# A two-layer hybrid decoder trunk: where weights are split, which banks the gates use, and when gated outputs are turned

## The chip, the cores and the metric

The kernel runs on one core of a Trainium2 chip. The metric is the device time of one execution in microseconds (us); three runs of the kernel before gave 1159.62 to 1160.34 us, with a median of 1159.97 us. Five engines share the work: TensorE (PE in the profile; PEld is its weight load), VectorE (DVE), ScalarE (ACT), GpSimd (POOL) and SyncE (SP), which here issues the transfers from device memory (DMA). Sums of products land in PSUM, in eight banks of 128 x 512 fp32 numbers.

## The reference

256 tokens of 1024 numbers pass through two layers. Each layer has a mixer and a mixture of experts:

```python
proj = h @ w_in[l]
(c_q, c_kv, k_rope, dn_qkv, dn_beta, dn_a, dn_gate,
 hg_q, hg_f, hg_i, hg_gate, gate_logits) = jnp.split(proj, SPLIT_POINTS, axis=-1)
y_a = mla_branch(c_q, c_kv, k_rope, ...) @ w_br_a[l]       # latent attention, 8 heads
y_b = gated_deltanet_branch(dn_qkv, ..., dn_gate, ...) @ w_br_b[l]
y_c = hgrn2_branch(hg_q, hg_f, hg_i, hg_gate, ...) @ w_br_c[l]
g_a, g_b, g_c = jnp.split(jax.nn.sigmoid(gate_logits), N_BRANCHES, axis=-1)
mixed = (g_a * y_a + g_b * y_b + g_c * y_c) @ w_out[l]
h = layer_norm(DEEPNORM_ALPHA * h + mixed, ln1_g[l], ln1_b[l])
moe_out = hier_moe(h, ...)         # top 1 of 4 groups, then top 2 of its 8 experts of width 256
h = layer_norm(DEEPNORM_ALPHA * h + moe_out, ln2_g[l], ln2_b[l])
```

The outputs of the deltanet and HGRN2 branches are normalised per head and multiplied by silu of their gates (dn_gate, hg_gate) before w_br_b and w_br_c.

## The kernel before

**Splitting.** The mixer's products keep fp32 precision by writing each operand as a high part (fp32r) and a remainder. For a weight piece of 128 x 1024, `split` (L241) makes the high part wh with a copy on ACT (L249) and the remainder wl with a subtraction (L250). The subtraction is on DVE, except for four pieces of a layer named in `POOLED` (L143), where POOL does it: both pieces of chunk cq (the first projection), one of the first merge gate, one of the deltanet gate. `mm3` then issues three products: high by high, high by low, low by high (L261 to L263). wh and wl have two buffers each.

**Layer.** A layer (L589) starts with the hidden state in token rows. Two diagonal matrices hold each token's 1/deviation (L619); multiplied by them on PE, the state is turned and scaled at once (L395), evacuated by ACT and DVE (L401, L403), and split into hTh and hTl (L254, L255). Then come the chunks of the input projection and the three branches in the order of the list `seq`, `merge_branch` a, the gates of both remaining branches, `branch_gate` (normalise, gate, turn the gated outputs by L1126), merges b and c, and `project_out` with the router's products. Weights arrive in tiles of 128 x 2048 fp32 (1 MB), four buffers at a time; when the mixer's pool `mp` closes, `open_prefetch` takes its memory for 13 tiles more, first the rest of the mixer's weights and then the first experts'.

**Banks.** A wide product (256 tokens x 512 columns) accumulates in two banks. `ps("pa")` hands out pa and po in turn; pb and pm have three banks each, which go to scans, turns and small sums. Every gate, merge and output product thus takes the pair pa, po, and the next one may start in a bank when DVE or ACT has read the last.

**Clock products.** `warm(n)` issues n bf16 products of 128 x 512 whose result nobody reads (L365). They stand after the turned state in layer 0 (8 of them) and at the end of layer 0's experts (14).

**Experts.** They run in quads, with 1 MB tiles of gate, up and down weights streaming in through rotating buffers (L1602, L1635). A scheduler orders each engine's instructions by the program's order and dependencies; `issue_after` keeps an instruction behind a given one.

## Time and profile before

| what | value |
|---|---|
| median of 3 runs | 1159.97 us |
| the profiled execution | 1160.61 us |
| its span | 1158.8 us |
| PE, DVE, ACT, POOL busy | 91%, 50%, 37%, 14% |
| mixer of layer 0, about | 0 to 376 us |
| experts of layer 0, about | 376 to 577 us |
| mixer of layer 1, about | 578 to 945 us |
| experts of layer 1, about | 945 to 1137 us |

An execution is 1.8 us longer than its span. A busy share is a mean over stages; so the stages are read apart. In a timeline, a bracket at a row's end tells how long the engine had been idle and what ended that. The matmuls' ends are modelled: in an unbroken row of 512-column products one lasts 0.40 us and the next starts 0.23 to 0.24 us after it, so an idle time in a bracket is 0.16 us shorter than what the start of the row was late.

### The profile page before, as it was taken

To read this page: it belongs to the slowest core of one execution; us is meant where nothing else is said; L and a number is where in the kernel's file an instruction comes from. 1 tells how busy PE (TensorE), PEld (TensorE's weight loads), DVE (VectorE), ACT (ScalarE), POOL (GpSimd) and SP (SyncE) were. 2 spreads that over 40 slices of the span, in tenths; PEclk is the share of its full clock that TensorE was granted. 3 is DMA by queue.
4 is the path that set the end of the run, shared out by engine and by line. 5 is a ranking of instruction groups with operands and counts; after the bars stand their busy time and mean duration, and the time that the engine had idled before them with its cause. 6 is when DMAs were issued, how large, how long until landed. Compare 5 with 4: busy or idle time off the path is not lost. (4 is left out here: it accounts for less than half of the span.)

```text
span 1158.8 us, 21407 instructions
## 1 busy us (share of the span) xinstructions
PE 1059.3 (91%) x8896; PEld 775.6 (67%) x8896; DVE 576.9 (50%) x1269; ACT 427.3 (37%) x788; POOL 162.7 (14%) x146
## 2 busy tenths in 40 slices
PE   7999999999999998777889999999999999977775
PEld 5888987777777664434378889777777766543442
DVE  7677754575556422111276876645754562321114
ACT  5764632554445211111067545235444351211111
POOL 2111025101210400000020110450021112000001
PEclk9999999999999999898899999999999999989997
DMA  7632250549965999999983214315599679999994
GB/s 231 200 107 73 91 165 2 169 158 359 424 271 220 410 425 426 426 426 427 366 230 106 74 46 138 110 38 182 196 411 374 251 270 425 426 425 426 427 426 190
DMA packets 104706, 305.58 MB, mean 264 GB/s; under 512 B 20962, under 2 KB 48028, under 8 KB 79516
## 3 DMA queue, kind: packets, MB, share of 16 engines
q1 hardware_dynamic: 104604, 304.15, 68.4%
q8 instruction: 72, 1.18, 0.4%
q14 instruction: 30, 0.25, 0.1%
HBM read 303.08 MB, written 1.05 MB: 262 GB/s over the span
## 5 line engine op out<-in xcount | busy, mean ns | idle before, releaser
L250 DVE TENSOR_TENSOR wl<-w,wh 128x1024 fp32r<-128x1024 f32 x150 | 187.0, 1248 | 161.5 <-ACT wh L249 161.0
L249 ACT CAST wh<-w 128x1024 fp32r<-128x1024 f32 x158 | 165.7, 1049 | 217.7 <-PE ps_po L263 74.7
L1602 PE MATMUL ps_pa<-w,xg 128*32 128x256 f32 x2304 | 175.1, 436 | 59.0 <-DMA w<-in_exp_w_up_dram 29.4
L1602 PEld LDWEIGHTS ps_pa<-w,xg 128*32 128x32 f32 x2304 | 88.0, 125 | 140.4 <-DMA w<-in_exp_w_up_dram 38.2
L1614 DVE SCALAR_TENSOR_TENSOR hm<-ps_pa,ws,hm 128x256 f32<-128x256 f32 x18 | 8.7, 484 | 203.5 <-ACT hm L1613 203.3
L1613 ACT ACTIVATE hm<-ps_pa 128x256 f32<-128x256 f32 x18 | 6.9, 384 | 221.8 <-PE ps_pa L1602 221.8
L261 PE MATMUL ps_pa<-wh,hTh 128*128 128x512 f32 x176 | 71.2, 405 | 2.0 <-ACT hTh L254 0.7
L261 PE MATMUL ps_po<-wh,hTh 128*128 128x512 f32 x176 | 71.2, 405 | 1.9 <-ACT hTh L254 0.7
L262 PE MATMUL ps_po<-wl,hTh 128*128 128x512 f32 x176 | 70.5, 401 | 2.1 <-DVE wl L250 1.6
L262 PE MATMUL ps_pa<-wl,hTh 128*128 128x512 f32 x176 | 70.5, 401 | 2.1 <-DVE wl L250 1.6
L1635 PE MATMUL ps_pm<-w,hmT 128*32 128x512 f32 x576 | 70.8, 595 | 1.3 <-issue 1.3
L263 PE MATMUL ps_pa<-wh,hTl 128*128 128x512 f32 x176 | 70.0, 398 | 0.2 <-DVE hTl L255 0.2
L263 PE MATMUL ps_po<-wh,hTl 128*128 128x512 f32 x176 | 69.9, 397 | 0.2 <-DVE hTl L255 0.2
L1552 PEld LDWEIGHTS ps_pm<-P,h1c 128*128 128x128 f32 x576 | 66.8, 192 | 2.2 <-ACT res L1350 1.0
L1552 PE MATMUL ps_pm<-P,h1c 128*128 128x128 f32 x576 | 67.3, 275 | 0.0
L1561 ACT ACTIVATE xg<-ps_pm,gb 128x128 f32<-128x128 f32 x72 | 32.9, 458 | 71.7 <-DVE xg L1559 71.7
L1574 POOL TENSOR_TENSOR Pw<-P,small 128x128 f32<-128x128 f32 x32 | 12.4, 405 | 306.9 <-PE ps_pm L1581 227.9
L1279 POOL TENSOR_TENSOR mix<-mix,sg 128x512 f32<-128x512 f32 x16 | 28.3, 1792 | 155.4 <-DVE sg L1277 155.4
L1559 DVE TENSOR_SCALAR xg<-ps_pm,gb 128x128 f32<-128x128 f32 x72 | 29.4, 408 | 41.2 <-PE ps_pm L1552 32.2
L263 PE MATMUL ps_po<-hTh,wl 128*128 128x256 f32 (+1 forms) x168 | 48.7, 290 | 0.9 <-DVE wl L250 0.5
L263 PE MATMUL ps_pa<-hTh,wl 128*128 128x256 f32 (+1 forms) x168 | 48.9, 291 | 0.5 <-DVE wl L250 0.5
L261 PE MATMUL ps_pa<-hTh,wh 128*128 128x256 f32 (+1 forms) x168 | 49.2, 293 | 0.0
(442 smaller groups left out, 2134.9 us busy)
## 6 DMA issues: line engine op xcount, KB each, us to landing
w<-in_exp_w_gate_dram SPq DMA_DIRECT2D x66, 1024.0 KB
w<-in_exp_w_up_dram SPq DMA_DIRECT2D x66, 1024.0 KB
w<-in_exp_w_down_dram SPq DMA_DIRECT2D x64, 1024.0 KB
w<-in_w_in_dram SPq DMA_DIRECT2D x58, 1024.0 KB
w<-in_w_out_dram SPq DMA_DIRECT2D x8, 1024.0 KB
w<-in_w_br_a_dram SPq DMA_DIRECT2D x4, 1024.0 KB
w<-in_w_br_b_dram SPq DMA_DIRECT2D x4, 1024.0 KB
w<-in_w_br_c_dram SPq DMA_DIRECT2D x4, 1024.0 KB
```

The costliest lines, as they stand in the source:

```text
L249: nc.scalar.copy(v(hi), raw)
L250: engine.tensor_tensor(v(lo), raw, v(hi).bitcast(F32), op=OP.subtract)
L261: mm(ps, a[0], b[0], start=start, stop=False, skip_group_check=True)
L262: mm(ps, a[0], b[1], start=False, stop=False, skip_group_check=True)
L263: mm(ps, a[1], b[0], start=False, stop=stop, skip_group_check=True)
L1279: nc.gpsimd.tensor_tensor(mv, mv, sg[t], op=OP.add)
L1552: nc.tensor.matmul(ps[:, 128 * k:128 * k + 128], xc[:, t, 4 * h + k], Ps[q][:, t], start=(t == 0), stop=(t == 1))
L1559: nc.vector.tensor_scalar(xg[:, k], o, g, b, op0=OP.mult, op1=OP.add)
L1561: nc.scalar.activation(xg[:, k], o, AF.Identity, scale=g, bias=b)
L1574: self.pool_last = nc.gpsimd.tensor_tensor(e(Pw[:, t]), e(P[:, t]), w, op=OP.mult)
L1602: nc.tensor.matmul(pg[32 * e:32 * e + 32, FF * n:FF * n + FF], xgs[q][k // 4][:, k % 4, 32 * e:32 * e + 32], w[:, FF * k:FF * k + FF], sta ...
L1635: nc.tensor.matmul(ps[c][32 * e:32 * e + 32], hmT[:, i, 32 * e:32 * e + 32], ws[e][:, D * i + 512 * c:D * i + 512 * c + 512], start=(i == ...
```

## The change

All remainders are subtracted on DVE (`POOLED` goes). At the beginning of layer 0 the 8 clock products go, and at its end 11 are left of 14; chunk cq is issued after the diagonal matrices. In layer 1, as in layer 0, the table of ACT for exp and ln is loaded at an earlier place, with the first exp of the decay right behind it. Once the scans are done, `pair` gives wide products the pair pa, po and a pair of pb in turn. `branch_gate` no longer turns its output: `branch_turned` does so after the first half gate of merge b. The router's column sums go from after the branch gates to after hg_project. `project_out` opens both output halves' pairs at once and computes first half of wo0, first half of wo1, second half of wo0, second half of wo1, with residual and router products in between.

```diff
-    POOLED = {"cq.0", "cq.1", "gla00.0", "dn_gate1.1"}
...
-    def split(self, raw, name):
+    def split(self, raw):
...
-        engine.tensor_tensor(v(lo), raw, v(hi).bitcast(F32), op=OP.subtract)
+        nc.vector.tensor_tensor(v(lo), raw, v(hi).bitcast(F32), op=OP.subtract)
...
     def wide(self, l, n, act):
-        ps = [self.ps("pa") for _ in range(TB)]
+        ps = self.pair()
...
+    def pair(self):
+        self.npair += 1
+        return [self.ps("pb" if self.scans_done and self.npair % 2 else "pa") for _ in range(TB)]
...
-                self.transposed(self.h, self.hT, self.gb0, ...)
+                self.hT_last = self.transposed(self.h, self.hT, self.gb0, ...)
                 if l == 0:
-                    with tc.issue_after(self.latest(self.nc.tensor)):
-                        self.warm(8)
...
-                self.chunk_cm(self.pq, l, "cq")
+                with tc.issue_after(self.diag):
+                    self.chunk_cm(self.pq, l, "cq")
...
+                    if n == "hg_project":
+                        self.router_sums(self.latest(self.nc.vector))
...
                 self.merge_branch(l, "a")
+                self.scans_done = True
                 self.gates(l, mp)
                 self.branch_gate(l, mp, "dn", self.dn_o)
                 self.branch_gate(l, mp, "hg", self.hg_o)
-                self.router_sums(self.last_gate.ins)
+                first = self.merge_gate(l, "b", 0)
+                self.bank = "pm"
+                self.branch_turned(l, "dn", self.dn_o)
+                self.branch_turned(l, "hg", self.hg_o)
+                self.bank = None
             self.pw = self.open_prefetch(f"prefetch{l}", self.NPRE)
-            self.merge_branch(l, "b")
+            self.merge_branch(l, "b", gate=first)
...
-        with self.tc.issue_after(self.last_sin.ins) if l == 0 else ExitStack():
+        with self.tc.issue_after(self.hT_last if l else self.last_sin.ins):
+            nexp = self.small([128, NH])
             self.tc.keep_in_program_order(nc.scalar.preload_act_table_set("natural_log_exp_and_others"))
+            nc.scalar.activation(nexp, self.alog, AF.Exp)
...
+        ps = [self.pair() for _ in range(2)]
+        for c in range(2):
+            self.wide_half(ps[c], l, f"wo{c}", self.mixS, 0)
+            if c == 0:
+                self.mix_turned(1)
+        self.wide_half(ps[0], l, "wo0", self.mixS, 1)
+        residual(0)
+        for t in range(TB):
+            route(t, 0)
+        self.wide_half(ps[1], l, "wo1", self.mixS, 1, True)
+        free()
+        residual(1)
+        for t in range(TB):
+            route(t, 1)
...
-            self.warm(14)
+            self.warm(11)
```

Three places show it in the engines' orders. The first is DVE at the beginning of layer 1, before: L338 to L344 are the last steps of the layer norm's 1/deviation, sg the diagonal matrices, L403 evacuates the turned state.

```order
L338 SCALAR_TENSOR_TENSOR ln_tmp<-ln_tmp 128x2
L340 TENSOR_SCALAR ln_rs<-ln_tmp,ln_rs 128x1 x2
L342 TENSOR_SCALAR ln_tmp<-ln_rs,ln_v_5356 128x1 x2
L344 TENSOR_SCALAR ln_rs<-ln_tmp,ln_rs 128x1 x2
L619 TENSOR_SCALAR sg<-const,ln_rs 128x128 x2
L403 TENSOR_SCALAR d_5437<-ps_pm,vcol_5038 128x256
L403 TENSOR_SCALAR d_5448<-ps_pm,vcol_5038 128x256 x2
L255 TENSOR_TENSOR hTl<-d_5437,hTh 128x512
L255 TENSOR_TENSOR hTl<-d_5448,hTh 128x512
```

The same place after (L621 was L619, L405 was L403, L252 was L255):

```order
L340 SCALAR_TENSOR_TENSOR ln_tmp<-ln_tmp 128x2
L342 TENSOR_SCALAR ln_rs<-ln_tmp,ln_rs 128x1 x2
L344 TENSOR_SCALAR ln_tmp<-ln_rs,ln_v_5344 128x1 x2
L346 TENSOR_SCALAR ln_rs<-ln_tmp,ln_rs 128x1 x2
L621 TENSOR_SCALAR sg<-const,ln_rs 128x128 x2
L247 TENSOR_TENSOR wl<-w,wh 128x1024
L405 TENSOR_SCALAR d_5425<-ps_pm,vcol_5027 128x256
L405 TENSOR_SCALAR d_5436<-ps_pm,vcol_5027 128x256 x2
L252 TENSOR_TENSOR hTl<-d_5425,hTh 128x512
L247 TENSOR_TENSOR wl<-w,wh 128x1024
L252 TENSOR_TENSOR hTl<-d_5436,hTh 128x512
```

Two subtractions of 128 x 1024 have come into DVE's row, one behind the diagonal matrices and one between the first two hTl.

The second place is PE from the end of the branch gates to merge b, before: d_2110 and a_2193 are the gated outputs that L1126 turns, "..." stands for ten products.

```order
L263 MATMUL ps_po<-wh,hTl 128x512
L1126 MATMUL ps_pb<-const,d_2110 128x128 x4
L1126 MATMUL ps_pm<-const,d_2110 128x128 x4
L1126 MATMUL ps_pb<-const,a_2193 128x128
L261 MATMUL ps_pa<-wh,hTh 128x512
L262 MATMUL ps_pa<-wl,hTh 128x512
L263 MATMUL ps_pa<-wh,hTl 128x512
...
L1126 MATMUL ps_pb<-const,a_2193 128x128 x3
L261 MATMUL ps_pa<-wh,hTh 128x512
L1126 MATMUL ps_pm<-const,a_2193 128x128 x3
L261 MATMUL ps_po<-wh,hTh 128x512
```

The same place after (L1140 was L1126, L258 to L260 were L261 to L263); "..." stands for thirty products of merge b's first half gate.

```order
L258 MATMUL ps_po<-wh,hTh 128x512
L258 MATMUL ps_pa<-wh,hTh 128x512
L1140 MATMUL ps_pm<-const,d_2109 128x128 x8
L1140 MATMUL ps_pm<-const,a_2192 128x128 x2
L259 MATMUL ps_po<-wl,hTh 128x512
L260 MATMUL ps_po<-wh,hTl 128x512
L258 MATMUL ps_po<-wh,hTh 128x512
...
L260 MATMUL ps_pa<-wh,hTl 128x512
L1140 MATMUL ps_pm<-const,a_2192 128x128 x6
L258 MATMUL ps_pb<-wh,o_2775 128x512
L259 MATMUL ps_pb<-wl,o_2775 128x512
```

The turns stood before the gate's products and among their first ones, in banks pb and pm; now they stand within the half gate and behind it, in pm, and merge b's product starts in pb right behind the last of them.

The third place is PE at the second turn of the merged rows (mix) in front of the output projection, before:

```order
L263 MATMUL ps_po<-wh,hTl 128x512
L1287 MATMUL ps_pb<-const,mix 128x128 x4
L1287 MATMUL ps_pm<-const,mix 128x128 x4
L261 MATMUL ps_pa<-wh,hTh 128x512
L262 MATMUL ps_pa<-wl,hTh 128x512
L261 MATMUL ps_po<-wh,hTh 128x512
L262 MATMUL ps_po<-wl,hTh 128x512
L263 MATMUL ps_pa<-wh,hTl 128x512
```

The same place after (L1306 was L1287):

```order
L260 MATMUL ps_pa<-wh,hTl 128x512
L1306 MATMUL ps_pm<-const,mix 128x128 x8
L258 MATMUL ps_pb<-wh,hTh 128x512
L259 MATMUL ps_pb<-wl,hTh 128x512
L260 MATMUL ps_pb<-wh,hTl 128x512
```

The eight turns take pm alone, and the output product behind them accumulates in pb, where it had the pair pa, po that the product in front of the turns had used.

## Rows read from the trace of the kernel before

**Rows 1.** Windows of the span: PE, PEld, DVE, ACT, POOL busy, PEclk, DMA share, GB/s

```profile
280.00:320.00 40.00, 39.70 (x168) 31.00 (x167) 19.97 (x18) 16.51 (x19) 7.08 (x4) 1.00 1.03 420
336.00:348.00 12.00, 10.80 (x44) 8.17 (x45) 7.65 (x10) 4.33 (x6) 0.00 (x0) 1.00 0.50 185
348.00:376.00 28.00, 27.98 (x234) 21.64 (x236) 18.25 (x91) 15.78 (x25) 0.84 (x2) 1.00 0.57 220
376.00:560.00 184.00, 154.62 (x1618) 89.56 (x1610) 44.54 (x103) 27.08 (x56) 16.35 (x24) 0.93 1.01 423
```

**Rows 2.** Timeline of PE, beginning of layer 1; start, length (us), line, result<-operands, [idle before]

```profile
578.98 3.18 PE L365 MATMUL ps_pa<-bits 128*128 128x512 bf16 x14 [0.30 <-DVE ln_rs L334]
...
585.17 3.03 PE L395 MATMUL ps_pm<-sg,res 128*128 128x128 f32 x16 [3.02 <-issue]
...
588.00 2.61 PE L395 MATMUL ps_pb<-sg,res 128*128 128x128 f32 x16
```

**Rows 3.** Timeline of DVE, same stretch

```profile
579.50 2.34 DVE L338 SCALAR_TENSOR_TENSOR ln_tmp<-ln_tmp 128x2 f32<-128x2 f32 x1
...
583.10 2.07 DVE L619 TENSOR_SCALAR sg<-const,ln_rs 128x128 f32<-128x128 f32 x2 [0.26 <-DMA mconst<-in_consts_dram]
```

**Rows 4.** Timeline of POOL, the whole span

```profile
11.14 5.13 POOL L250 TENSOR_TENSOR wl<-w,wh 128x1024 fp32r<-128x1024 f32 x2 [9.35 <-ACT wh L249]
...
276.20 3.54 POOL L1279 TENSOR_TENSOR mix<-mix,sg 128x512 f32<-128x512 f32 x2 [35.27 <-DVE sg L1277]
...
579.47 2.35 POOL L250 TENSOR_TENSOR wl<-w,wh 128x1024 fp32r<-128x1024 f32 x1
...
582.54 2.34 POOL L250 TENSOR_TENSOR wl<-w,wh 128x1024 fp32r<-128x1024 f32 x1 [0.72 <-ACT wh L249]
```

**Rows 5.** Page's section 5, VectorE's remainders: count | busy us, mean ns | idle before

```profile
L250 DVE TENSOR_TENSOR wl<-w,wh 128x1024 fp32r<-128x1024 f32 x150 | 187.0, 1248 | 161.5 <-ACT wh L249 161.0
```

**Rows 6.** Timeline of DVE, beginning of layer 0

```profile
8.47 0.16 DVE L338 SCALAR_TENSOR_TENSOR ln_tmp<-ln_tmp 128x2 f32<-128x2 f32 x1
...
9.54 0.47 DVE L619 TENSOR_SCALAR sg<-const,ln_rs 128x128 f32<-128x128 f32 x2
...
13.26 3.56 DVE L255 TENSOR_TENSOR hTl<-d,hTh 128x512 fp32r<-128x512 f32 x2
...
17.65 0.67 DVE L255 TENSOR_TENSOR hTl<-d,hTh 128x512 fp32r<-128x512 f32 x1
```

**Rows 7.** Timeline of PE, beginning of layer 0

```profile
10.36 1.95 PE L395 MATMUL ps_pm<-sg,res 128*128 128x128 f32 x16
...
13.93 1.89 PE L365 MATMUL ps_pa<-bits 128*128 128x512 bf16 x8
...
16.88 0.39 PE L262 MATMUL ps_pm<-hTl,wh 128*128 128x256 f32 x1 [0.22 <-DVE hTl L255]
...
28.83 0.67 PE L702 MATMUL ps_pb<-d,mconst 64*128 64x256 f32 x2 [1.49 <-DVE lb_e L530]
```

**Rows 8.** Windows of 4 and 3 us, columns as in rows 1

```profile
29.00:33.00 4.00, 4.00 (x17) 3.47 (x17) 2.02 (x12) 1.42 (x4) 0.00 (x0) 0.57 0.88 203
585.00:588.00 3.00, 2.83 (x17) 2.86 (x17) 0.70 (x2) 2.08 (x4) 0.00 (x0) 0.66 0.67 142
```

**Rows 9.** Timeline of PE, gates, merges and output projection of layer 0

```profile
240.98 0.50 PE L262 MATMUL ps_pa<-wl,hTh 128*128 128x512 f32 x1 [0.56 <-POOL wl L250]
...
261.92 0.50 PE L262 MATMUL ps_pa<-wl,hTh 128*128 128x512 f32 x1 [1.56 <-DVE wl L250]
...
276.27 0.47 PE L261 MATMUL ps_pa<-wh,hTh 128*128 128x512 f32 x1 [0.18 <-DVE sg L1277]
...
336.74 0.50 PE L261 MATMUL ps_pa<-wh,hTh 128*128 128x512 f32 x1 [0.75 <-ACT hTh L254]
```

**Rows 10.** Timeline of DVE, gates and merge b of layer 0

```profile
259.51 1.22 DVE L568 TENSOR_REDUCE rsum<-rw 128x72 f32<-128x576 f32 x1
...
277.21 1.37 DVE L250 TENSOR_TENSOR wl<-w,wh 128x1024 fp32r<-128x1024 f32 x1 [0.40 <-ACT wh L249]
```

More of the change, by code (lines that the diff above doesn't have):

```diff
@@ L238, in done @@
             self.issue(pool)
-    def split(self, raw, name):
+    def split(self, raw):
         nc = self.nc
-        engine = nc.gpsimd if name in self.POOLED else nc.vector
         hi = self.sp.tile([128, 1024], F32R, name="wh", tag="wh", bufs=self.NB["wh"])
@@ L269, in dense_cm @@
         for k0 in range(0, nk, ku):
-            w = self.split(raw[:, k0:k0 + ku], f"{name}.{k0 // ku}")
+            w = self.split(raw[:, k0:k0 + ku])
             for b in range(nb):
@@ L281, in dense_tm @@
             if j not in w:
-                w[j] = self.split(raw[:, j:j + 2], f"{name}.{j // 2}")
+                w[j] = self.split(raw[:, j:j + 2])
             for k in range(2):
@@ L591, in layer @@
         with ExitStack() as cl, ExitStack() as cr:
-            self.ctx_l = cl
+            self.ctx_l, self.scans_done = cl, False
             self.sp = cr.enter_context(tc.tile_pool(name=f"split{l}", bufs=1, **side))
@@ L618, in layer @@
                 for t in range(TB):
[L619 to L620 removed]
+                    i = self.nc.vector.tensor_scalar(diag[:, t], self.ident, self.hrs[:, t], None, op0=OP.mult)
+                self.diag = i.ins
+                self.hT_last = self.transposed(self.h, self.hT, self.gb0, tmp=lambda: self.buf("d2", [128, 2, T]), scale=diag)
                 if l == 0:
[L622 to L623 removed]
                     with tc.issue_after(self.last_lo.ins):
@@ L717, in dn_decay @@
         nc.vector.scalar_tensor_tensor(x, a, 0.0, x, op0=OP.max, op1=OP.add)
-        nexp = self.small([128, NH])
-        nc.scalar.activation(nexp, self.alog, AF.Exp)
         nc.vector.scalar_tensor_tensor(g, x, -1.0, nexp[:, None, :].to_broadcast([128, TB, NH]), op0=OP.mult, op1=OP.mult)
@@ L1118, in branch_gate, with branch_turned @@
         for i in range(8):
-            self.last_gate = nc.vector.scalar_tensor_tensor(ov[:, i], ov[:, i], rs[:, i:i + 1], gv[:, i], op0=OP.mult,
-                                                            op1=OP.mult)
+            nc.vector.scalar_tensor_tensor(ov[:, i], ov[:, i], rs[:, i:i + 1], gv[:, i], op0=OP.mult, op1=OP.mult)
+    def branch_turned(self, l, n, o):
+        nc = self.nc
         oT = self.o4()
@@ L1257, in mla_heads, with merge_gate, merge_branch @@
             self.dump_oT(l, "mla")
-    def merge_branch(self, l, br, between=None):
+    def merge_gate(self, l, br, c):
+        sg = [self.gp.tile([128, 512], F32, name="sg", tag="sg", bufs=self.NB["sg"]) for _ in range(TB)]
+        for s, ps in zip(sg, self.wide(l, f"gl{br}{c}", self.hT)):
+            self.nc.scalar.activation(s, ps, AF.Tanh, scale=0.5)
+        return sg
+    def merge_branch(self, l, br, between=None, gate=None):
         nc = self.nc
@@ L1265, in merge_branch @@
         for c in range(2):
-            sg = [self.gp.tile([128, 512], F32, name="sg", tag="sg", bufs=self.NB["sg"]) for _ in range(TB)]
-            for s, ps in zip(sg, self.wide(l, f"gl{br}{c}", self.hT)):
-                nc.scalar.activation(s, ps, AF.Tanh, scale=0.5)
+            sg = gate if gate and c == 0 else self.merge_gate(l, br, c)
             if c and between:
@@ L1271, in merge_branch @@
             n = f"br_{br}{c}"
-            ps = [self.ps("pa") for _ in range(TB)]
+            ps = self.pair()
             self.dense_tm(ps, self.w(l, n).rearrange("p (k c) -> p k c", k=4), oT, n, 0, 4)
@@ L1294, in project_out @@
         r, st = self.h, self.stats(2)
+        self.bank = "pm"
         pr = self.ps()
@@ L1306, in route, with residual @@
                                  start=(t + c + k == 0), stop=(c + k == 4), skip_group_check=True)
-        for c in range(2):
-            ps = [self.ps("pa") for _ in range(TB)]
-            for i in range(2):
-                self.wide_half(ps, l, f"wo{c}", self.mixS, i, c + i == 2)
-                if c == 0 and i == 0:
-                    self.mix_turned(1)
-                if c == 1 and i == 0:
-                    for t in range(TB):
-                        route(t, 0)
-            if c:
-                free()
+        def residual(c):
             cs = slice(512 * c, 512 * c + 512)
             for t in range(TB):
-                nc.vector.scalar_tensor_tensor(r[:, t, cs], self.h[:, t, cs], 2 * ALPHA, ps[t], op0=OP.mult, op1=OP.add)
+                nc.vector.scalar_tensor_tensor(r[:, t, cs], self.h[:, t, cs], 2 * ALPHA, ps[c][t], op0=OP.mult, op1=OP.add)
                 nc.vector.bn_stats(st[:, t, c], r[:, t, cs])
+        ps = [self.pair() for _ in range(2)]
[10 more added lines that the diff above has]
+        residual(1)
         for t in range(TB):
             route(t, 1)
-        self.logits, self.st1 = pr, st
+        self.logits, self.st1, self.bank = pr, st, None
     def router(self, l, ep, x, xc):
```

4 lines of the change are left out of this document (1 added, 3 removed).

## The prediction

> **What bounds the kernel now.** I read the windows by stage first. In the mixer PE is the bound: it is busy in 39.70 of 40 us in the merges, while the transfer engines, full there, have slack in the two windows behind [rows 1]. In the experts it is the other way round: 184 us with a DMA share of 1.01 and PE busy for 154.62 us [rows 1]. So a mixer's time is PE's instructions plus the places where PE waits, and an experts' stage ends with its weights. Whether time gained in a mixer is kept depends on the stream: between 336 and 376 us the share is 0.50 and 0.57, which leaves 12 x 0.50 + 28 x 0.43 = 18 us in which it stands still, because the prefetched tiles are full and their readers have not come [rows 1]. The stream then goes on when the experts' first quad gives tiles back, and that comes earlier if the mixer ends earlier. I therefore count every microsecond that PE gains in a mixer as one of the end. After the windows I read the timelines of PE for rows with an idle time, and at each the timeline of the engine that released it.
>
> **Beginning of layer 1.** PE's 14 clock products start at 578.98 and take 3.18 us; then it is idle for 3.02 us until the turned state (L395) at 585.17 [rows 2]. What is late is VectorE: L338, two numbers per partition, takes 2.34 us, and L619, two diagonal matrices, 2.07 us [rows 3]; the same instructions take 0.16 and 0.47 us at layer 0's beginning [rows 6]. Both stand beside POOL's subtractions at 579.47 and 582.54, and L338 ends when the first of these does (579.50 + 2.34 against 579.47 + 2.35) [rows 3, 4]. With these subtractions gone from POOL, (2.34 - 0.16) + (2.07 - 0.47) = 3.78 us of DVE's chain go, and L395 starts at about 581.4, when 11 clock products have just ended. In the window 585 to 588 the granted clock is 0.66, a mixture of 1.2 and 2.4 GHz [rows 8], and the two blocks of 16 turns take 3.03 and 2.61 us [rows 2] against 1.95 us at layer 0's beginning [rows 7]: behind a pause of 3 us PE turns at the lower level. Without the pause I take the higher one, (3.03 - 1.95) + (2.61 - 1.95) = 1.7 us more. Against these 5.5 us stand two subtractions that DVE now does, 1.25 us each [rows 5]. The first stands in front of the first evacuation and lies mostly beside the first turns; the second stands between the first two hTl and delays the second, which chunk cq's products wait for. I put both at 1.4 us on the path: 5.5 - 1.4 = 4.1 us. The bounds: 5.5 if PE never meets the subtractions; if the clock stays low and both stand on the path whole, 3.78 - 2.5 = 1.3. ACT's table load, which stood between its first evacuation and its first cast, goes behind the casts, beside another one; PE has its second block of turns meanwhile, so I give nothing for it.
>
> The Trainium skill's page "SBUF — State Buffer" ("Who interferes with whom") says that VectorE and GpSimd share one port pair, that an instruction of VectorE with two inputs in SBUF contends with a GpSimd instruction that reads SBUF, and that the one which comes second "fully blocks". L338 beside POOL's row agrees. The same rule speaks against the change: a subtraction moved to VectorE has two such inputs, and would wait for whole instructions of what POOL keeps. The trace bears that out little where it matters: the subtraction at 277.21 takes 1.37 us [rows 10] beside POOL's pair of products of 3.54 us from 276.20 [rows 4]. By the rule alone it would cost up to 1.77 us more, half of that pair, at each of a layer's merges where they meet; by the row 0.12 us more than the mean [rows 5]. I go by the row.
>
> **Beginning of layer 0.** POOL's two subtractions run from 11.14 to 16.27 [rows 4], and DVE's pair of hTl beside them takes 3.56 us, where a single one behind them takes 0.67 [rows 6]; PE waits for hTl until 16.88 [rows 7]. So 3.56 - 2 x 0.67 = 2.2 us go from DVE's chain, the subtraction that comes in between the two costs 1.25 of them [rows 5], and the one ahead of them a part of the rest: I take 0.4 us. The 8 clock products of 1.89 us [rows 7] fill a time in which PE waits for the split state anyway, so that by themselves they give nothing. Later PE waits 1.49 us at L702 for VectorE's small instructions [rows 7], and in the 4 us behind that the granted clock is 0.57, near the lower level [rows 8]: 4 x (1 - 0.57) = 1.7 us of work are lost. DVE's queue ahead of L702 changes, and the order puts some 27 products and one row of sums ahead of it, which cover that wait; but the next row of sums waits for an activation of ACT behind the tables of angles, and I think that more than half of the 3.2 us appears there again. I take 1.3 us, together 1.7. Bounds: 0.4 + 3.2 = 3.6 us; and -1 us if PE, without the clock products, runs the first products at the lower level. The row for that price is the turned state at layer 1's beginning, 3.03 - 1.95 = 1.08 us for one block [rows 2, 7].
>
> **Gates, merges and output projection, in each layer.** Each idle time costs 0.16 us more than its bracket shows.
> - At 240.98 PE waits 0.56 us for POOL's subtraction [rows 9]; on VectorE it is half as long [rows 4, 5] and ready in time: 0.7 us.
> - At 261.92 it waits 1.56 us for a subtraction on VectorE [rows 9]. That one stood behind the gating of the branch outputs and the router's reduction of 1.22 us [rows 10]. The reduction goes to hg_project, and behind the gates now stands a half gate whose products need no gated output: 1.7 us.
> - At 276.27 a gate's first product waits 0.18 us for a bank that VectorE is still reading [rows 9]; it is the first of four such places in merges b and c, and with two pairs of banks each wait has a whole product of 11 us to end in. Four times 0.3 is 1.2 us.
> - At 336.74 the output product waits 0.75 us for the split of the turned rows [rows 9]. PE is idle for 12 - 10.80 = 1.2 us from 336 to 348 [rows 1], this place and two smaller ones, with 3 x 0.16 = 1.7 us. Afterwards the first halves of both outputs give PE other products before it needs the second turn, and route and residual lie between halves of different banks: 1.7 us, of which a part can come back where the turn's eight products take one tag alone.
> Together 5.3 us a layer. The new order also makes new waits: ten places a layer (turns in pm alone, eight evacuations behind them, DVE with four more subtractions, the router's sums in hg_project) where what ended second now ends last. I estimate 0.1 us for each, 1.0 us a layer. Bounds for a layer: 5.3 with none; 2.3 if each costs what the merges' waits cost, 0.3. DVE itself has room: 19.97 of 40 us in the merges [rows 1].
>
> **What else moves.** The mixer's pool closes behind the last turn, about 4 us later against the gates than before, and the tiles behind it are asked for later. Merge b's first weights lie in the four buffers ahead, the next are needed a product (11 us) later, and the prefetch has its 18 us [rows 1]. I cost it at nothing. Without the slack it would be 4 us a layer.
>
> **The sum.** 4.1 + 1.7 + 2 x (5.3 - 1.0) = 14.4 us. The profiled execution took 1160.6 us, its span of 1158.8 and 1.8 around it: 1160.6 - 14.4 = 1146.2. The median of the runs is 0.6 us lower than that execution, so I predict 1145.5 us. With the terms' bounds: all upper ones, 5.5 + 3.6 + 10.6 = 19.7, 1140; all lower ones, 1.3 - 1 + 4.6 = 4.9, 1155.
>
> **Rivals.**
> - *Waits change place.* Each place that PE waited at gets another last releaser: VectorE, with eight more subtractions and 10 us more work, is late behind the turns and the residual. For it speaks that VectorE ended most of the waits [rows 7, 9]; against it that it is half idle in the merges [rows 1]. Then the layers give half, and layer 0's beginning nothing: 4.1 + 4.3 = 8.4 us, 1151.5.
> - *The stream takes it back.* If the experts' stage waited for the stream from its first tile on, a shorter mixer would only make it wait longer, and the end would move by 1 us or less: 1159. Against it stand the 18 us of slack [rows 1].
> - *Slower by the clock.* The first products of both layers run at 1.2 GHz, because there are fewer clock products in front of them and PE has short pauses. A granted clock of 0.57 costs 0.43 us of each us [rows 8]. Of the gains 3.8 us of DVE's chain and 8.6 of the layers would be left, 12.4; so it decides from 12.4 / 0.43 = 29 us at the lower level, some 15 at each beginning. With 20 at each it costs 17 us, and the kernel is 4.6 us slower: 1164.5. Against it: behind the pauses of before, 3.02 and 1.49 us, the clock was low for some 4 to 6 us, not 15 [rows 2, 7, 8]. The Trainium skill's page "TensorE: Matmul & The Clock Gate" ("What's actually happening") says that the throttled state is the default and that activity releases it; the pause in front of the 0.66 agrees, and by that rule fewer clock products are a risk.
> - *More than summed.* The wait at L702 and the slow stretch behind it go whole, 1.9 us more, no new wait comes, 2.0, and layer 1's subtractions stay off the path, 1.4: 1140.2.
>
> **Chances.** The forecast 0.66, waits change place 0.17, the stream 0.05, the clock 0.05, more than summed 0.07. The forecast's own range is 1141 to 1150; for 8 in 10, with the second and a part of the last case, 1139 to 1154. A measurement here tells about 0.2% (2.3 us) from no change: faster 0.91 (first, second and last case and a little of the third), the same 0.04, slower 0.05.
>
> **What would show it.** L338 and L619 at layer 1's beginning at 0.2 and 0.5 us, no 3 us of idle on PE there, and both blocks of turns at 1.95 us with a granted clock of 1.00; if the clock is 0.66 or below there, 1.7 us of the sum are wrong. In the merges no wait for a bank in front of a gate; in front of the output projection none over 0.3 us. The wait behind the branch gates gone; if one for VectorE stands at the turns, the second case is true. PE's rows of layer 0's stages from 40 us on should stand about 1.7 us earlier than before, those of the experts of layer 0 about 6 us, and those of layer 1's experts 14 us. The forecast is wrong if the experts' first quad, so shifted, waits for transfers that it did not wait for.

## The result and the profile after

The changed kernel takes 1142.24 us (median of four runs, 1140.55 to 1143.08), the kernel before 1159.80 us beside it: a ratio of 0.9848, 95% interval 0.9835 to 0.9862, or 16 to 19 us. I had predicted 1145.5 us: the time lies in the range, 3.3 us below the forecast.

The same instructions of PE in both traces tell where it came from. The profiled execution is the fastest of the four (1140.55 us), and the one before took 1160.61 us, so the stages add up to 20.0 us and not to 17.6.

| stretch, up to the start of | before, after (us) | gained in it | forecast |
|---|---|---|---|
| layer 0's beginning, to the scores L1185 (now L1199) | 38.95, 35.91 | 3.0 | 1.7 |
| rest of layer 0's mixer, to L1552 (L1575) | 367.64, 358.97 | 5.6 | 4.3 |
| layer 0's experts, to the last row of L1635 (L1658) | 568.73, 559.28 | 0.8 | 0 |
| layer 1's beginning, to L702 (L716) | 600.30, 587.01 | 3.8 | 4.1 |
| rest of layer 1's mixer, to L1552 (L1575) | 937.65, 918.07 | 6.3 | 4.3 |
| layer 1's experts, to the last row of L1635 (L1658) | 1138.84, 1118.85 | 0.4 | 0 |

Layer 1's beginning on PE (timeline, columns as in [rows 2]): the turned state no longer stands behind 3 us of idle, but behind 0.38 us that ACT ends, and its blocks take 2.02 and 1.95 us.

```profile
569.53 2.53 PE L367 MATMUL ps_pa<-bits 128*128 128x512 bf16 x11 [0.30 <-DVE ln_v L335]
...
572.44 2.02 PE L397 MATMUL ps_pm<-sg,res 128*128 128x128 f32 x16 [0.38 <-ACT res L356]
...
574.30 1.95 PE L397 MATMUL ps_pb<-sg,res 128*128 128x128 f32 x16
...
577.89 0.39 PE L259 MATMUL ps_pm<-hTl,wh 128*128 128x256 f32 x1 [0.69 <-DVE hTl L252]
```

The same stretch on DVE, against [rows 3]: L340 was L338, L621 was L619.

```profile
570.19 0.16 DVE L340 SCALAR_TENSOR_TENSOR ln_tmp<-ln_tmp 128x2 f32<-128x2 f32 x1
...
571.95 0.48 DVE L621 TENSOR_SCALAR sg<-const,ln_rs 128x128 f32<-128x128 f32 x2 [0.61 <-DVE ln_rs L346]
...
576.01 1.22 DVE L247 TENSOR_TENSOR wl<-w,wh 128x1024 fp32r<-128x1024 f32 x1
...
577.15 1.30 DVE L252 TENSOR_TENSOR hTl<-d,hTh 128x512 fp32r<-128x512 f32 x2
```

2.34 and 2.07 us have become 0.16 and 0.48. The new cost is here too: the remainder at 576.01 stands in front of the second hTl, and PE waits 0.69 us for that at 577.89.

Layer 0's beginning on PE, against [rows 7]:

```profile
10.55 1.95 PE L397 MATMUL ps_pm<-sg,res 128*128 128x128 f32 x16
...
12.33 1.95 PE L397 MATMUL ps_pb<-sg,res 128*128 128x128 f32 x16
...
16.04 0.39 PE L259 MATMUL ps_pm<-hTl,wh 128*128 128x256 f32 x1 [0.76 <-DVE hTl L252]
...
29.11 0.70 PE L1188 MATMUL ps_pm<-a,ones 128*128 128x256 f32 x2 [0.74 <-ACT a L1184]
...
29.74 0.70 PE L716 MATMUL ps_pb<-d,mconst 64*128 64x256 f32 x2
```

Chunk cq's wait for hTl has grown from 0.22 to 0.76 us, but cq also started 1.4 us earlier, without the clock products. A wait of before that the prediction does not list has gone too:

```profile
22.73 0.34 PE L263 MATMUL ps_po<-hTh,wl 128*72 128x256 f32 x1 [0.45 <-DVE wl L691]
```

L716 (was L702) does not wait; L1188 ahead of it does, for ACT, 0.74 us. What follows is the surprise against [rows 8] (windows of the changed kernel; PEclk, the granted clock, is the third number from the end):

```profile
27.00:31.00 4.00, 3.26 (x18) 2.27 (x17) 3.79 (x14) 3.49 (x8) 0.00 (x0) 1.00 0.76 172
31.00:35.00 4.00, 4.00 (x36) 4.00 (x35) 2.86 (x19) 1.62 (x6) 1.04 (x1) 1.00 0.82 199
```

The clock stays at 1.00, where the pause of before was followed by 0.57. In the gates, merges and the output projection no wait of [rows 9] is left; only one of PE's rows from 240 to 345 us shows an idle time (layer 1 has the same one, 0.46 us at 832.68):

```profile
273.59 0.50 PE L259 MATMUL ps_po<-wl,hTh 128*128 128x512 f32 x1 [0.47 <-DVE wl L247]
```

It is new, and its reason stands in the rows of DVE (first fence) and POOL (second fence) beside it:

```profile
271.19 2.34 DVE L247 TENSOR_TENSOR wl<-w,wh 128x1024 fp32r<-128x1024 f32 x1 [0.40 <-ACT wh L246]
...
288.89 1.41 DVE L247 TENSOR_TENSOR wl<-w,wh 128x1024 fp32r<-128x1024 f32 x1 [0.40 <-ACT wh L246]
```

```profile
269.90 2.55 POOL L1298 TENSOR_TENSOR mix<-mix,sg 128x512 f32<-128x512 f32 x2 [64.94 <-DVE sg L1296]
...
287.91 3.54 POOL L1298 TENSOR_TENSOR mix<-mix,sg 128x512 f32<-128x512 f32 x2 [15.46 <-DVE sg L1296]
```

The remainder at 271.19 takes 2.34 us instead of 1.23: it came while POOL was in the second of two products, which ended at 272.45, 1.1 us ahead of the remainder's end. At 288.89 it takes 1.41, and there POOL's pair takes 3.54 us instead of 2.55. One of the two engines waits each time.

Windows of the transfers' slack, for [rows 1]:

```profile
328.00:340.00 12.00, 12.00 (x57) 9.77 (x56) 6.02 (x7) 5.17 (x6) 0.00 (x0) 1.00 0.70 265
340.00:368.00 28.00, 27.98 (x242) 20.92 (x244) 19.96 (x95) 15.79 (x25) 0.81 (x2) 1.00 0.58 214
368.00:552.00 184.00, 157.41 (x1616) 90.00 (x1611) 44.55 (x103) 27.11 (x56) 16.36 (x24) 0.91 1.01 423
```

12 x 0.30 + 28 x 0.42 = 15.4 us of idle transfers are left where there were 18; the stream is full from the same point in the program on.

### The profile page after: what moved, and what is told of

It is laid out like the page before. It is cut to its first block, busy times and chain, and to the rows that moved or that the text cites. A ratio compares the mean times of both kernels' runs of the same rounds, so it can differ in the third digit from the quotient of the medians.

```text
span 1138.8 us, 21371 instructions
## 1 busy us (share of the span) xinstructions
PE 1054.5 (93%) x8885; PEld 776.4 (68%) x8885; DVE 582.3 (51%) x1277; ACT 425.9 (37%) x787; POOL 140.8 (12%) x138
## 5 line engine op out<-in xcount | busy, mean ns | idle before, releaser
L247 DVE TENSOR_TENSOR wl<-w,wh 128x1024 fp32r<-128x1024 f32 x158 | 198.3, 1257 | 144.2 <-ACT wh L246 141.4
L1625 PE MATMUL ps_pa<-w,xg 128*32 128x256 f32 x2304 | 179.6, 448 | 52.5 <-DMA w<-in_exp_w_up_dram 25.8
L1625 PEld LDWEIGHTS ps_pa<-w,xg 128*32 128x32 f32 x2304 | 90.9, 128 | 135.5 <-issue 37.4
L1658 PE MATMUL ps_pm<-w,hmT 128*32 128x512 f32 x576 | 71.6, 595 | 1.3 <-issue 1.3
L1575 PEld LDWEIGHTS ps_pm<-P,h1c 128*128 128x128 f32 x576 | 66.8, 192 | 2.2 <-ACT res L1373 1.0
L1575 PE MATMUL ps_pm<-P,h1c 128*128 128x128 f32 x576 | 67.3, 275 | 0.0
L259 PE MATMUL ps_pb<-wl,hTh 128*128 128x512 f32 x128 | 51.0, 398 | 0.5 <-DVE wl L247 0.5
L260 PE MATMUL ps_pb<-wh,hTl 128*128 128x512 f32 x128 | 50.8, 397 | 0.0
L258 PE MATMUL ps_pb<-wh,hTh 128*128 128x512 f32 x128 | 50.4, 398 | 0.0
L1658 PEld LDWEIGHTS ps_pm<-w,hmT 128*32 128x32 f32 x576 | 21.1, 109 | 41.4 <-issue 31.9
L252 DVE TENSOR_TENSOR Yl<-ps_pm,Yh 128x512 fp32r<-128x512 f32 x36 | 24.8, 688 | 47.8 <-ACT Yh L251 47.8
L258 PE MATMUL ps_po<-hTh,wh 128*128 128x256 f32 (+1 forms) x168 | 49.2, 293 | 0.0
L260 PE MATMUL ps_po<-hTh,wl 128*128 128x256 f32 (+1 forms) x168 | 48.7, 290 | 0.5 <-DVE wl L247 0.5
L260 PE MATMUL ps_pa<-hTh,wl 128*128 128x256 f32 (+1 forms) x168 | 48.6, 290 | 0.5 <-DVE wl L247 0.5
L258 PE MATMUL ps_pa<-hTh,wh 128*128 128x256 f32 (+1 forms) x168 | 48.7, 290 | 0.1
```

What stands on the lines that cost most here:

```text
L247: nc.vector.tensor_tensor(v(lo), raw, v(hi).bitcast(F32), op=OP.subtract)
L252: self.last_lo = (engine or self.nc.vector).tensor_tensor(lo, src, hi.bitcast(F32), op=OP.subtract)
L258: mm(ps, a[0], b[0], start=start, stop=False, skip_group_check=True)
L259: mm(ps, a[0], b[1], start=False, stop=False, skip_group_check=True)
L260: mm(ps, a[1], b[0], start=False, stop=stop, skip_group_check=True)
L1575: nc.tensor.matmul(ps[:, 128 * k:128 * k + 128], xc[:, t, 4 * h + k], Ps[q][:, t], start=(t == 0), stop=(t == 1))
```

## The experiments

Each kernel is the changed one with one edit. The times are medians; stage times come from one profiled execution each. Apart from the edits, the start of layer 0's turned state lies up to 1.1 us later from one execution to the next, which is taken off where stages are compared.

| run | median (us) | ratio to the kernel before, 95% interval |
|---|---|---|
| the changed kernel | 1142.24 | 0.9848, 0.9835 to 0.9862 |
| POOL's load alone | 1150.11 | 0.9920, 0.9895 to 0.9946 |
| four remainders back on POOL | 1158.89 | 0.9998, 0.9983 to 1.0013 |
| clock products back | 1144.56 | 0.9867, 0.9851 to 0.9884 |
| no clock products, layer 1 | 1142.73 | 0.9865, 0.9842 to 0.9889 |
| table load back | 1144.07 | 0.9872, 0.9856 to 0.9889 |
| sums back | 1147.76 | 0.9899, 0.9873 to 0.9924 |
| turns back | 1141.65 | 0.9844, 0.9824 to 0.9863 |
| one pair of banks | 1146.29 | 0.9883, 0.9866 to 0.9900 |
| output order back | 1144.41 | 0.9876, 0.9857 to 0.9894 |
| shorter mixer | 1118.39 | 0.9644, 0.9626 to 0.9662 |
| later remainder | 1143.71 | 0.9865, 0.9848 to 0.9881 |
| later remainder, pause filled | 1143.22 | 0.9860, 0.9844 to 0.9877 |

Of differences of 2 us the intervals overlap; there the stages decide.

**POOL's load alone.** POOL makes chunk cq's remainders a second time, into a tile that nobody reads. All rows of DVE, ACT and PE stand in the same order as in the changed kernel.

```diff
             w = self.split(raw[:, k0:k0 + ku])
+            if name == "cq":
+                x = self.sp.tile([128, 1024], F32, name="wx", tag="wx", bufs=1)...
+                self.nc.gpsimd.tensor_tensor(x, raw[:, k0:k0 + ku], w[0].bitcast(F32), op=OP.subtract)
```

> The changed kernel, with POOL making chunk cq's two remainders of each layer a second time, into a tile that nobody reads. Every instruction of VectorE, ACT and PE stands in the order of the changed kernel, so that only POOL's work beside them is new. Theory (POOL's subtractions hold up VectorE): at layer 1's beginning the step of 128 x 2 numbers takes 2.3 us instead of 0.16 and the diagonal matrices 2.1 instead of 0.5, the turned state comes 3.8 us later and at the lower clock; at layer 0's beginning VectorE's subtractions and hTl wait for POOL too, 2 us or more. At layer 1's products some 5 to 6 us later than in the changed kernel, in all 6 to 8 us slower, 1148 to 1150. Rival (the kernel with POOL's subtractions was slow because the scheduler ordered the rest otherwise): VectorE's rows keep their lengths, less than 1 us, 1143.

Measured: 7.9 us slower than the changed kernel. In the profiled execution 3.4 us are lost by layer 0's chunk ckv and 3.6 by layer 1's chunk cq; another 1.6 are lost at 51 us, where the granted clock falls behind a pause on PE that the changed kernel has as well (below, one pair of banks), and I don't count them as the load's. DVE, then POOL:

```profile
10.96 1.22 DVE L247 TENSOR_TENSOR wl<-w,wh 128x1024 fp32r<-128x1024 f32 x1 [1.02 <-ACT wh L246]
...
14.63 2.75 DVE L252 TENSOR_TENSOR hTl<-d,hTh 128x512 fp32r<-128x512 f32 x1
...
576.33 2.17 DVE L343 SCALAR_TENSOR_TENSOR ln_tmp<-ln_tmp 128x2 f32<-128x2 f32 x1
...
584.09 1.76 DVE L252 TENSOR_TENSOR hTl<-d,hTh 128x512 fp32r<-128x512 f32 x1
```

```profile
11.07 5.77 POOL L270 TENSOR_TENSOR wx<-w,wh 128x1024 f32<-128x1024 f32 x2 [9.28 <-ACT wh L246]
...
576.13 2.35 POOL L270 TENSOR_TENSOR wx<-w,wh 128x1024 f32<-128x1024 f32 x1
...
582.95 2.35 POOL L270 TENSOR_TENSOR wx<-w,wh 128x1024 f32<-128x1024 f32 x1 [4.47 <-ACT wh L246]
```

L343 (was L340) lasts until POOL's product ends, at 578.5. The hTl at 584.09 ends at 585.85, 0.55 us behind POOL's next product (585.30); one alone takes 0.67 [rows 6]. The diagonal matrices, free of POOL here, stay at 0.48 us. At 10.96 DVE was first by 0.1 us: its remainder takes 1.22, and POOL's pair 5.77 instead of the 5.13 of [rows 4]. The theory holds: with the order of every other engine unchanged, DVE's waits are POOL's doing.

**Four remainders back on POOL.**

```diff
+    POOLED = {"cq.0", "cq.1", "gla00.0", "dn_gate1.1"}
...
+        engine = nc.gpsimd if name in self.POOLED else nc.vector
```

> The changed kernel with four remainders of a layer back on POOL (both of chunk cq, one of the first merge gate, one of the deltanet gate). Theory: POOL's subtraction holds up short VectorE instructions beside it. At layer 1's beginning the step of 128 x 2 numbers takes 2.3 us again and the diagonal matrices 2.1, and the turned state on PE starts about 3.8 us later at the lower clock; in layer 0 the pair of hTl takes 3.5 us again; at each layer's deltanet gate PE waits 0.6 us. About 6.5 us slower than the changed kernel (1142.2), 1148.7. Rival: the beginnings gained by the order of chunk cq and the table load, not by the port; then only the two gates' waits come back, 1.4 us, 1143.6.

Measured: no gain over before is left; the theory missed by 10 us and the rival by 15. The scheduler orders hundreds of DVE's and PE's rows otherwise, so the run can't price the four pieces. The beginnings lose 1.5 us in layer 0 and 2.3 in layer 1, where L342 (L338 before) takes 2.18 us again, and PE waits 0.57 and 0.55 us at the deltanet gates, as expected. What the theory had left out stands elsewhere: PE waits 2 us at L1039 in each layer, and 3.0 us at L867 in layer 1, where the changed kernel waits 0.8. These are waits for POOL too. DVE, then POOL, ahead of L1039:

```profile
164.94 3.56 DVE L1061 TENSOR_TENSOR a<-a 128x256 f32<-128x256 f32 x2
```

```profile
162.93 3.74 POOL L249 TENSOR_TENSOR wl<-w,wh 128x1024 fp32r<-128x1024 f32 x1 [46.48 <-ACT wh L248]
```

The remainder at 162.93 is the first merge gate's, one of the four pieces; the two steps of DVE beside it (128x256, then 128x128) take 0.43 and 0.28 us in the changed kernel. Ahead of L867 two products of POOL stand that another order put there, and DVE's L311 takes 1.00 us beside them instead of 0.16. In the kernel before the same remainder stood on POOL, and PE had no such wait. So what a piece on POOL costs hangs on what the order puts beside it, and how the 16.6 us divide between the port and the order stays open. An edit undone in a scheduled kernel undoes more than itself; for the price at the beginnings the experiment above stands.

**Clock products.** Back at both beginnings, and taken away at layer 1's:

```diff
+                    with tc.issue_after(self.latest(self.nc.tensor)):
+                        self.warm(8)
...
-            self.warm(11)
+            self.warm(14)
```

> The changed kernel with 8 clock products at layer 0's beginning and 14 instead of 11 at layer 1's. Theory: they stand on PE's path now. Chunk cq, which starts at 14.04 us, starts 1.6 us later, and layer 1's turned state 0.6 us later: 2.2 us slower, 1144.4. Rival of the prediction (fewer clock products lower the clock): they give back the time that they take, and the kernel is not slower, 1142 or less.

Measured: 2.3 us slower, near the theory's 2.2, but in layer 0 by another way. Chunk cq starts 2.0 us later there; its wait for hTl is gone in exchange, and 0.8 us are left at the end of the chunks. Then PE waits 1.20 us at L718, where the changed kernel waited 0.74 at L1188, and the clock falls behind that (window of this kernel; 1.00 in the changed one):

```profile
31.00:35.00 4.00, 3.46 (x16) 3.00 (x17) 3.35 (x20) 2.87 (x9) 0.00 (x0) 0.73 1.06 255
```

With this it is 2.0 us again by 52 us. Layer 1's turned state starts 0.1 us later, not 0.6; its beginning loses 0.7 at chunk cq, where PE waits 0.46 us for ACT's and 0.81 for DVE's split in the order that the scheduler made anew. So the eight products themselves cost 0.8 us, nothing was gained by having them, and that the whole came out as expected is luck.

```diff
-            self.warm(11)
```

> The changed kernel without the 11 clock products at layer 1's beginning. Theory: behind a pause of some 3 us PE turns the state at the lower level, 3.0 and 2.6 us for the two blocks instead of 2.0 each, granted clock 0.6 to 0.8 there: 1.7 us slower, 1143.9. Rival: PE's clock is held by the experts' last products, and nothing changes, 1142.2.

Measured: a time that the runs can't tell from the changed kernel's. The stage can (timeline, then windows):

```profile
573.36 3.52 PE L397 MATMUL ps_pm<-sg,res 128*128 128x128 f32 x16 [3.21 <-DVE sg L621]
...
576.68 2.12 PE L397 MATMUL ps_pb<-sg,res 128*128 128x128 f32 x16
```

```profile
573.00:576.00 3.00, 2.64 (x13) 2.67 (x14) 2.03 (x4) 1.65 (x4) 0.00 (x0) 0.60 1.13 319
576.00:579.00 3.00, 3.00 (x25) 3.00 (x24) 2.08 (x4) 1.51 (x4) 0.00 (x0) 0.83 0.74 152
```

Behind a pause of 3.21 us the first block takes 3.52 us at a granted clock of 0.60, and layer 1's first product of cq comes 1.6 us later. So the 11 products are worth 1.6 us in the stage, as expected. The beginning of before, with its pause of 3.02 us and a first block of 3.03 us [rows 2], fits this.

**The table load.**

```diff
-        with self.tc.issue_after(self.hT_last if l else self.last_sin.ins):
-            nexp = self.small([128, NH])
+        with self.tc.issue_after(self.last_sin.ins) if l == 0 else ExitStack():
...
-            nc.scalar.activation(nexp, self.alog, AF.Exp)
...
+        nexp = self.small([128, NH])
+        nc.scalar.activation(nexp, self.alog, AF.Exp)
```

> The changed kernel with the load of ACT's table and the exp of the decay's factor at their old places. In layer 1 the load of 1.28 us then stands where the scheduler puts it, before as between ACT's first evacuation and its first cast. Theory of the prediction: PE has its second block of turns meanwhile, 0 us, 1142.2. Rival: with the pause on PE gone the first cast is what PE's chunk cq waits for, and the load comes on the path, 1.3 us, 1143.5.

Measured: 1.8 us slower, but neither expectation's way. Layer 1's beginning is 0.3 us later. The rest is layer 0's: 3.2 us by 52 us, where PE waits 3.0 instead of 1.4 us at the first attention head's turns and the clock falls to 0.50 behind that. What the load itself costs stays open, since the edit moved the order there too.

**The router's sums and the turns,** back to their places, one at a time:

```diff
-                    if n == "hg_project":
-                        self.router_sums(self.latest(self.nc.vector))
...
                 self.branch_gate(l, mp, "hg", self.hg_o)
+                self.router_sums(self.latest(self.nc.vector))
```

> The changed kernel with the router's column sums back behind the branch gates. Theory of the prediction: the reduction of 1.2 us stands in VectorE's queue ahead of a remainder that PE waits for, and part of the wait of 1.56 us before comes back: 0.5 to 1.2 us a layer, 1143.2 to 1144.6. Rival (the turns behind the half gate cover it): nothing, 1142.2.

Measured: 5.5 us slower, more than either expectation. In layer 0 a wait comes back behind the reduction, but the one of 0.47 us at 273.59 goes, and next to nothing is lost in all:

```profile
256.98 0.49 PE L259 MATMUL ps_po<-wl,hTh 128*128 128x512 f32 x1 [0.71 <-DVE wl L247]
```

In layer 1 6.2 us are lost. PE, DVE and windows there:

```profile
813.26 0.59 PE L1139 MATMUL ps_pm<-const,a 128*128 128x128 f32 x3 [1.24 <-DVE a L1130]
...
816.37 0.70 PE L573 MATMUL ps_pb<-rsum,ones 128*128 128x72 f32 x2 [2.52 <-DVE rsum L571]
```

```profile
812.33 1.65 DVE L1130 SCALAR_TENSOR_TENSOR a<-a,small,a 128x128 f32<-128x128 f32 x6
...
813.91 1.17 DVE L570 TENSOR_REDUCE rsum<-rw 128x72 f32<-128x576 f32 x1
...
815.00 1.21 DVE L247 TENSOR_TENSOR wl<-w,wh 128x1024 fp32r<-128x1024 f32 x1
...
816.13 0.18 DVE L571 TENSOR_TENSOR rsum<-rsum,rb 1x36 f32<-1x36 f32 x1
```

```profile
814.00:817.00 3.00, 0.64 (x3) 0.64 (x4) 2.97 (x4) 0.57 (x1) 0.00 (x0) 0.82 0.00 0
817.00:820.00 3.00, 3.00 (x9) 2.32 (x9) 1.55 (x3) 0.00 (x0) 0.00 (x0) 0.50 0.89 268
820.00:823.00 3.00, 3.00 (x9) 2.38 (x8) 0.00 (x0) 0.69 (x1) 0.00 (x0) 0.55 0.24 87
```

The sums (L573) stand in PE's row behind the turns, and wait 2.52 us for the reduction and a remainder ahead of it on DVE; with the wait before, PE pauses 3.8 us, and then works for some 6 us at 0.50 to 0.55. A wait of 3.8 us costs 6.2.

```diff
-                first = self.merge_gate(l, "b", 0)
                 self.bank = "pm"
-                self.branch_turned(l, "dn", self.dn_o)
...
+                first = self.merge_gate(l, "b", 0)
```

(each `branch_turned` then stands behind its `branch_gate`.)

> The changed kernel with the gated outputs turned right behind the branch gates, ahead of merge b's first half gate in the program. Theory: the turns wait for VectorE's gating, and PE with them or the remainders behind them: 1 to 1.7 us a layer between gates and merge b, 1144.2 to 1145.6. Rival (the scheduler's order, not the place in the program, decides, or the sums made the wait): under 0.3 us a layer, 1142.5.

Measured: the same as the changed kernel. A wait for a remainder comes back behind the gates of each layer, and the one of 0.47 at 273.59 goes:

```profile
256.92 0.50 PE L259 MATMUL ps_po<-wl,hTh 128*128 128x512 f32 x1 [0.46 <-DVE wl L247]
```

The move of the turns gave nothing in all once the sums were away. Both in their old places together were not run.

**Banks and the output projection.**

```diff
-        return [self.ps("pb" if self.scans_done and self.npair % 2 else "pa") for _ in range(TB)]
+        return [self.ps("pb" if self.owo and self.npair % 2 else "pa") for _ in range(TB)]
```

(`owo` is set in front of the output projection alone.)

> The changed kernel with the pair pa, po alone for gates and merges b and c; the output projection keeps two pairs. Theory: the four waits for a bank at merges b and c come back, 0.3 us each, 1.2 us a layer, 1144.6 in all. Rival (the remainders of the next piece end later than the bank): under 0.3 us a layer, 1142.5.

Measured: 4.1 us slower. The gates and merges lose 1.6 us in layer 0 and 1.7 in layer 1, over the expected 1.2. In the profiled execution, the slowest of the four, another 1.5 us were lost at 47 us, in rows that are those of the changed kernel; windows of this kernel, then of the changed one:

```profile
47.00:50.00 3.00, 2.09 (x14) 1.57 (x14) 2.41 (x7) 2.98 (x7) 0.00 (x0) 0.87 0.44 156
50.00:53.00 3.00, 3.00 (x14) 2.37 (x11) 1.66 (x6) 1.05 (x2) 0.00 (x0) 0.56 0.00 0
```

```profile
44.00:47.00 3.00, 1.73 (x15) 1.56 (x14) 1.74 (x13) 2.77 (x11) 0.00 (x0) 1.00 1.02 361
47.00:50.00 3.00, 2.82 (x20) 2.04 (x20) 2.53 (x6) 2.99 (x5) 0.00 (x0) 1.00 0.04 15
```

The pause of 1.27 us in front of the attention's turns is the same in both; in one execution the clock falls behind it, in the other it doesn't.

```diff
-        for c in range(2):
-            self.wide_half(ps[c], l, f"wo{c}", self.mixS, 0)
-            if c == 0:
-                self.mix_turned(1)
+        self.wide_half(ps[0], l, "wo0", self.mixS, 0)
+        self.mix_turned(1)
         self.wide_half(ps[0], l, "wo0", self.mixS, 1)
         residual(0)
+        self.wide_half(ps[1], l, "wo1", self.mixS, 0)
```

> The changed kernel with the output projection's four half products in the old order (wo0 first, wo0 second, wo1 first, wo1 second half), still with two pairs of banks. Theory of the prediction: the first half of wo1 covers the split of the second turn and the residual; without it PE waits again 0.9 us behind the turn and 0.35 for its low part, 1.2 us a layer, 2.4 us slower, 1144.6. Rival (the two pairs of banks brought it): under 0.3 us a layer, 1142.5.

Measured: 2.2 us slower, as the theory says, and the two waits are those expected:

```profile
330.07 0.50 PE L258 MATMUL ps_po<-wh,hTh 128*128 128x512 f32 x1 [0.75 <-ACT hTh L251]
...
331.44 0.50 PE L260 MATMUL ps_po<-wh,hTl 128*128 128x512 f32 x1 [0.19 <-DVE hTl L252]
```

0.75 + 0.16 + 0.19 + 0.16 = 1.3 us in a layer.

**A shorter mixer.**

```diff
-        mm(ps, a[1], b[0], start=False, stop=stop, skip_group_check=True)
+        if not self.two:
+            mm(ps, a[1], b[0], start=False, stop=stop, skip_group_check=True)
```

(`two` is set for the gates of merges b and c alone.)

> The changed kernel without the third of the three products in the gates of merges b and c: 64 products of 128 x 512 fewer a layer, 15 us of PE at 0.234 us each. Theory (time gained in a mixer is kept until the transfers' idle time, some 15 us a layer between 328 and 368 us, is used up): the experts of both layers start 15 us earlier each, and the end comes 26 to 30 us earlier, 1112 to 1116. Rival of the prediction (the stream takes it back): the experts' stage becomes longer by half of it or more, and the end comes 15 us or less earlier, 1127 or more.

Measured: 23.9 us faster, less than the theory's 26 to 30 and far from the rival's 15. PE has 15 us less to do in a layer and gains 12 of them, since remainders (waits of 0.3 to 0.5 us) and POOL's merged rows (1.3 us) now end last at some places; in layer 0 the clock takes 1.4 us of the 12, behind the pause at 47 us. What is gained the experts keep to within a microsecond (9.0 us ahead at layer 0's last L1658 against 9.8 in front of the experts, 21.8 against 21.2 in layer 1).

```profile
328.00:348.00 20.00, 20.00 (x117) 14.29 (x116) 13.70 (x52) 10.04 (x12) 0.00 (x0) 1.00 0.92 362
348.00:360.00 12.00, 11.98 (x166) 10.38 (x163) 7.32 (x44) 6.75 (x15) 0.84 (x2) 1.00 0.49 188
360.00:540.00 180.00, 152.43 (x1573) 87.47 (x1570) 44.44 (x103) 27.11 (x56) 16.37 (x24) 0.92 1.01 424
```

The transfers are idle for 20 x 0.08 + 12 x 0.51 = 7.7 us of the slack, half of what they were: gained time uses it up, and the stream does not take it back.

**A version that should be faster.** The second remainder of cq behind the second hTl; and with it five products of 128 x 128 in the attention's pause.

```diff
-        nc.vector.tensor_tensor(v(lo), raw, v(hi).bitcast(F32), op=OP.subtract)
+        with self.tc.issue_after(after) if after else ExitStack():
+            nc.vector.tensor_tensor(v(lo), raw, v(hi).bitcast(F32), op=OP.subtract)
```

> The changed kernel with the second remainder of chunk cq put behind the second hTl in VectorE's row, where it stands between the first two. In the changed kernel PE waits 0.76 and 0.69 us there for hTl. Theory: these waits go, 0.9 us at each layer's beginning, 1.8 us faster, 1140.4. Rival (the remainder is then late itself, or the scheduler's other order costs as much elsewhere): no faster, 1142 or more.

```diff
+                if l == 0 and g == 0 and t == 0:
+                    ps = self.ps()
+                    for _ in range(5):
+                        nc.tensor.matmul(ps[:, 0:128], self.ident, P[:, 128:256], start=True, stop=True)
```

> The kernel with the later remainder and, in layer 0's first attention head, five products of 128 x 128 that nobody uses in PE's pause of 1.3 us in front of L1260, where in some executions the granted clock falls to 0.5 for 3 us and in others stays at 1.00. Theory (the pause lets the clock fall by chance, and that spreads the times of the changed kernel over 2.5 us): the fall does not come, the times lie closer together, and the median is 0.5 to 1 us below that of the kernel with the later remainder. Rival (another cause of the spread): no difference beyond 0.3 us, or slower by up to 0.5 us for the products.

Measured: 1143.71 and 1143.22 us. Neither beats the changed kernel. The theory's step came: the waits for hTl got shorter or went, and the beginnings are 0.6 us ahead at 24 us in layer 0 and 0.7 in layer 1. But the scheduler moved many other rows with it. In layer 0 PE waits 1.09 us instead of 0.74 for ACT at 29.50 and 0.33 at L718, and the clock falls behind that (window of the later remainder; 1.00 in the changed kernel):

```profile
31.00:35.00 4.00, 4.00 (x20) 3.65 (x21) 3.37 (x19) 2.08 (x7) 0.37 (x1) 0.63 0.88 216
```

That makes 0.6 us ahead into 1.6 behind at the scores, and PE waits 0.8 to 0.9 us more at each of two places of the first attention heads. With the five products the times differ by 0.5 us, within their spread, and the execution without them kept its clock behind the pause of 1.27 us: whether the pause makes the changed kernel's spread stays open.

## Why the prediction was right, and where it was off

- *Layer 1's beginning* (forecast 4.1, measured 3.8): right in mechanism and size. Of the 3.8 us of DVE's chain 3.3 came at the turned state, where ACT ends last now; the blocks gave the 1.7 forecast for the clock; the remainders took 1.1 us instead of 1.4. POOL's load alone brings L343 back to 2.17 us, the clock is 1.00 without the pause, and a pause of 3.21 us makes 3.52 us of a block again.
- *Layer 0's beginning* (1.7, measured 3.0): the split state was worth 0.9 us by the end of chunk cq, where I had 0.4. I had put the clock products at nothing, since they "fill a time in which PE waits for the split state anyway"; put back, they cost 0.8 us there, nearly all of the gain. The wait of 0.45 us at 22.73, which I had not counted, gave 0.7. And of the 3.2 us at L702 I expected more than half at the next row of sums; 0.74 us came there, the clock did not fall, and 1.7 were gained by the scores instead of 1.3. (The turned state itself started 0.2 us later.)
- *Gates, merges, output projection* (5.3 a layer less 1.0 for new waits; the rest of the mixers measured 5.6 and 6.3, 0.2 and 0.4 of it ahead of the gates): the named waits went, and the shares that runs show stand: pairs 1.6 and 1.7 us (forecast 1.2), output order 1.3 and pairs the rest of 1.7. The 1.0 for new waits came nearly whole, as two waits of 0.27 and 0.64 us in a layer. It was paid by what I had left out: smaller waits behind each of the large ones, about 0.1 us apiece, and 0.45 us in the router's products. That the sum stood in spite of it is luck.
- *The wait behind the gates* (1.7) was put down to the reduction and the turns alike. The runs don't divide it: with the sums' old place alone 0.71 us of it come back in layer 0 and another wait that costs 6.2 us in layer 1, with the turns' old place alone 0.46 in each layer. In the time the turns' move gave nothing, since a wait of 0.47 us came for it.
- *The port.* Here my reading of the row was wrong. From 1.37 us beside POOL's 3.54 I took that a remainder on VectorE hardly waits for POOL. The 3.54 was POOL's wait for VectorE: alone the pair takes 2.55 us. Where POOL comes first, once in a layer, the remainder takes 2.34 us and PE starts 0.64 us late. That price belonged into the sum by itself; it came as one of the two new waits. The Trainium skill's page "SBUF — State Buffer" ("Who interferes with whom") says that the port pair of the two engines is an exclusive lock and that issue order decides who blocks. Both rows of this case agree with it: DVE's 2.34 us where POOL was first, POOL's 3.54 where DVE was.
- *The stream* (nothing taken back): right; the shorter mixer shows it with 12 us a layer more. The 0.8 and 0.4 us of the experts are within what that stage varies by.
- *The clock rival:* didn't come. The pauses in front got shorter, 0.38 us for 3.02 in layer 1 and 0.74 for 1.49 in layer 0, and the granted clock behind the one in layer 0 is 1.00 in both windows. It was near: with waits of 1.20 and 1.09 us at that place of layer 0 (clock products back, later remainder) the clock fell.

## What to carry to other kernels

Work on GpSimd beside VectorE is not free even where GpSimd stands idle otherwise: here it made 2.17 us of a step of 0.16 in a serial chain, and of two long instructions on the two engines the later one waited. So a row's length beside such work is not the price for either. Count a pause of TensorE by what follows it too: pauses of 3.2 and 3.8 us cost 1.6 and 2.4 us more at the lower clock. In a kernel ordered by a scheduler, test a resource by adding load that moves no row, since undoing an edit reorders the rest and may cost more than what it is to measure.
